# First stage and DeltaNet of an encoder block: tensor work of GpSimd given to VectorE and ScalarE

## The chip, the cores and the metric

The kernel runs on one core of one Trainium2 chip. The metric is device time in microseconds (us), as the median of several runs. Of the kernel before there are three: 1435.29, 1437.44 and 1438.14 us, median 1437.44.

The engines are named as the profile names them: PE is TensorE (matmuls), PEld its weight loads, DVE is VectorE, ACT is ScalarE, POOL is GpSimd, SP is SyncE, which issues nearly all transfers here. Each engine takes its instructions strictly in order; semaphores make one wait for another. An instruction that stands at the head of its engine and waits holds back everything behind it.

## The reference

One encoder block over 256 tokens of width 2048. Two branches read the normalized input: a gated DeltaNet with 8 heads of 128 channels, run forwards and backwards, and a Fourier mixer. Their gated sum goes through an output projection; a squared-ReLU MLP of width 8192 follows. All weights are float32.

```python
h = rms_norm(x, g_mix)
q, k, v, z, f, scal, gates = split(h @ w_in)
q, k, v = split(silu(centred_short_conv(concat(q, k, v), conv_w)))
# per head and direction, in log decay g (<= 0) and beta:
#   S_t = exp(g_t) S_{t-1} (I - beta_t k_t k_t^T) + beta_t v_t k_t^T,  o_t = S_t q_t
y_a = (head_norm(o_fwd + o_bwd) * silu(z)) @ w_dn_up
y_f = real(fft2(f)) @ w_fourier
x = x + (sigmoid(gate_a) * y_a + sigmoid(gate_f) * y_f) @ w_o
x = x + relu(rms_norm(x, g_mlp) @ w_mlp_up) ** 2 @ w_mlp_down
out = rms_norm(x, g_final)
```

## The kernel before

**Weights and precision.** Every weight is streamed from memory once, in tiles of 512 KB (`raw`, four buffers). `split` (L87) turns each into two parts: ACT rounds it to the matmul's format (`hi`, L88), DVE subtracts to get the remainder (`lo`, L92). A product is three matmuls: hi by hi, hi by lo, lo by hi. So each 512 KB costs ACT one instruction of 128x1024, DVE one of 128x1024, and PE 24 matmuls 256 wide or 12 matmuls 512 wide. `pair_fm` (L104) and `tile_fm` (L131) make feature-major tiles, `stream` (L155) makes token-major columns.

**First stage** (`stream_k0`, L224). The transposed input arrives two k-tiles at a time (`xts`). `h_piece` (L188) multiplies it by the norm weights `gm` and splits it (`hh`, both parts); the first four tiles of k are accumulated as the pieces arrive. `h_square` (L203) squares the piece on ACT and adds it on POOL to `acc`, from which `finish_rstd` (L211) makes the reciprocal norms.

**Scalars** (L246 to L307). A small projection gives beta and the decay of each token and head. Softplus is a polynomial on 128x32 elements. Its result `g` is kept in two parts, `g_hi` and `g_lo`.

**DeltaNet.** The heads are done in two groups of four (`dn_group`, L615). In each group `dn_decay` (L425) builds the decay matrices E: eight operand tiles `A` (128x512, the triangular mask U times a per-token scalar, L435) go through matmuls (L436) and an exponential. `dn_k`, `dn_v`, `dn_q` project, convolve (`qkv_chunk`, L310: four dependent instructions on DVE per 128x256, L329) and normalize. `dn_inv` (L446) needs the inverse of unit triangular matrices of 128 rows, 16 per group. It takes their 64 diagonal blocks of 32x32, writes them to memory (`Kc`, L477) and reads them back one per partition (`Mf`, L483), inverts them by back substitution (`Xf`, L486 to L491: 31 steps of a product and a sum), writes `Xf` out (L493) and reads it back as `Xc` (L497). Matmuls then join 32-blocks to 64 (L518 to L529) and 64 to 128 (L537 to L542), giving `DT`. `dn_out` (L557) uses `DT`: a chain of small matmuls (L571, L577, L584, L590, L593, L598) with an eviction on DVE or ACT between each two, and the per-head norm on ACT and POOL.

**What is shared.** The temporary of the substitution, `tf`, has the tag `ti`; so have the temporaries of every second tile of the gate projection (L655), which follows the DeltaNet. The gates' results `merged` occupy the memory of the first group's E, Kt and Y. So the gate tiles can be multiplied into PSUM (four banks), but the first of them leaves PSUM only after the second group's substitution has ended and the first group's `dn_out` has read Y.

**What sets the order.** A scheduler orders each engine's instructions before the run by a simulated timeline (`schedule_with_timeline_sim`, L23). It moves work of one group between that of another. Constants and a few matmuls keep the program's order.

```python
for b in range(31, 0, -1):
    wd = 32 - b
    t3 = tf[:, 0:b * wd].rearrange("p (a c) -> p a c", a=b)
    pool.tensor_tensor(t3, Mf[:, 0:b, b:b + 1].to_broadcast([64, b, wd]),
                       Xf[:, b:b + 1, b:32].to_broadcast([64, b, wd]), op=ALU.mult)
    pool.tensor_tensor(Xf[:, 0:b, b:32], Xf[:, 0:b, b:32], t3, op=ALU.add)
```

## Time and profile before

| | |
|---|---|
| median of three runs | 1437.44 us (1435.29 to 1438.14) |
| span of the profiled execution | 1435.3 us |
| instructions of the program in it | 21399 |
| bytes moved | 255.19 MB, mean 178 GB/s |

The profiled execution has no time of its own beside its span; the span lies 2.1 us below the median and at the lowest of the three runs. What else is used of the profile stands in the prediction. A row of a group gives line, engine, operation, output and inputs, shape and count; then busy time in us, the mean of one in ns, and the idle time before them with what ended it. A row of a timeline gives start and length in us and how many instructions it joins. Durations of neighbouring instructions on one engine overlap a little, so the pitch from start to start is shorter than the duration.

For orientation in time: the first stage ends at 37.7 us; the first group's substitution runs from 119.3 to 184.9 us on POOL, the second group's from 224.3 to 278.3 us; the second z chunk's matmuls (L167) run from 231.8 to 262.3 us; the gate tiles from 267.5 to 386.9 us.

### The profile page before, as it was taken

How to read it: one execution, taken by the hardware profiler on the slowest of the kernel's cores; microseconds unless marked ns; L12 is line 12 of the kernel's file. 1: busy time of each engine (PE TensorE's matmuls, PEld its weight loads, DVE VectorE, ACT ScalarE, POOL GpSimd, SP SyncE). 2: the span in 40 equal slices, each digit the busy share in tenths (PEclk: the TensorE clock that was granted, in tenths of full speed). 3: DMA queues.
4: the chain of work that ended last, by engine and by line, in shares of the span. 5: the costliest groups of instructions: out<-in, count | busy, mean ns of one | idle time of the engine just before them, and what ended most of it. 6: DMA issues, size and time to landing. Idle time of an engine off the chain costs nothing.

```text
span 1435.3 us, 21399 instructions
## 1 busy us (share of the span) xinstructions
PE 1400.2 (98%) x8446; PEld 1235.3 (86%) x8446; DVE 904.4 (63%) x1136; ACT 679.4 (47%) x1017; POOL 189.4 (13%) x241
## 2 busy tenths in 40 slices
PE   8999799899999999999999999999999999999997
PEld 7989789688898899988888888888888888888897
DVE  8898888566655656656566666444446666645553
ACT  5545354455534444445554445333334454434442
POOL 8466926601000000000000000000000000000000
PEclk9999989999999999999999999999999999999999
DMA  7545344344556445576655556666665555666663
GB/s 239 167 155 165 100 136 121 114 139 144 189 179 201 162 158 186 183 257 200 189 182 187 188 187 184 195 196 191 192 192 188 187 186 185 191 191 193 193 198 121
DMA packets 85973, 255.19 MB, mean 178 GB/s; under 512 B 17008, under 2 KB 25200, under 8 KB 85488
## 3 DMA queue, kind: packets, MB, share of 16 engines
q1 hardware_dynamic: 84880, 249.62, 55.8%
q10 hardware_dynamic: 992, 4.19, 0.8%
q8 instruction: 66, 1.08, 0.3%
q14 instruction: 35, 0.29, 0.1%
HBM read 250.64 MB, written 3.15 MB: 177 GB/s over the span
## 4 chain that ended last, share of the span: by engine, by line
PE 83%; POOL 9%; DMA 3%; DVE 2%; issue 2%; ACT 1%; SPq 0%; POOLq 0%; ACTq 0%
PE mm L146 25%; PE mm L145 12%; PE mm L816 8%; PE mm L817 8%; PE mm L818 8%; POOL Xf L491 3%; PE mm L121 3%; PE mm L122 3%; PE mm L127 3%; PE mm L168 3%; PE mm L169 3%; PE mm L167 3%; POOL tf L489 3%; DVE lo L92 1%; DMA raw<-in_w_o_dram 1%
## 5 line engine op out<-in xcount | busy, mean ns | idle before, releaser
L92 DVE TENSOR_TENSOR lo<-raw,hi 128x1024 fp32r<-128x1024 f32 (+1 forms) x459 | 577.1, 1258 | 358.2 <-ACT hi L88 350.9
L88 ACT ACTIVATE hi<-raw 128x1024 fp32r<-128x1024 f32 (+1 forms) x459 | 485.5, 1059 | 436.5 <-PE mm L818 185.8
L146 PE MATMUL mm<-hh,hi 128*128 128x512 f32 x1536 | 539.5, 399 | 3.3 <-ACT hi L88 3.3
L145 PE MATMUL mm<-hh,lo 128*128 128x256 f32 x1440 | 405.8, 282 | 0.9 <-DVE lo L92 0.9
L146 PEld LDWEIGHTS mm<-hh,hi 128*128 128x128 f32 x1536 | 283.8, 189 | 65.0 <-ACT hi L88 3.5
L145 PEld LDWEIGHTS mm<-hh,lo 128*128 128x128 f32 x1440 | 273.1, 190 | 5.2 <-DVE lo L92 1.2
L817 PE MATMUL mm<-lo,rh 128*128 128x512 f32 (+1 forms) x512 | 192.3, 376 | 0.0
L818 PE MATMUL mm<-hi,rl 128*128 128x512 f32 (+1 forms) x512 | 192.3, 376 | 0.0
L816 PE MATMUL mm<-hi,rh 128*128 128x512 f32 (+1 forms) x512 | 173.7, 376 | 0.0
L867 POOL TENSOR_TENSOR rs<-rs,pex 128x1 f32<-128x1 f32 x2 | 1.1, 553 | 1082.0 <-DVE rs L866 1082.0
L818 PEld LDWEIGHTS mm<-hi,rl 128*128 128x128 f32 x512 | 96.4, 188 | 17.6
L816 PEld LDWEIGHTS mm<-hi,rh 128*128 128x128 f32 x512 | 96.2, 188 | 17.5
L817 PEld LDWEIGHTS mm<-lo,rh 128*128 128x128 f32 x512 | 96.3, 188 | 17.3
L127 PE MATMUL mm<-hh,lo 128*128 128x256 f32 x320 | 94.0, 294 | 1.0 <-DVE lo L92 1.0
L122 PE MATMUL mm<-hh,hi 128*128 128x256 f32 x320 | 94.0, 294 | 0.0
L121 PE MATMUL mm<-hh,hi 128*128 128x256 f32 x320 | 93.9, 293 | 0.0
L152 ACT COPY rt<-mm 128x256 f32<-128x256 f32 x64 | 23.9, 373 | 109.1 <-PE mm L146 109.1
L127 PEld LDWEIGHTS mm<-hh,lo 128*128 128x128 f32 x320 | 64.3, 201 | 1.4 <-DVE lo L92 1.2
L122 PEld LDWEIGHTS mm<-hh,hi 128*128 128x128 f32 x320 | 64.5, 202 | 0.5
L121 PEld LDWEIGHTS mm<-hh,hi 128*128 128x128 f32 x320 | 64.5, 202 | 0.2
L153 DVE TENSOR_TENSOR rt<-mm,rt 128x256 f32<-128x256 f32 x64 | 27.2, 425 | 55.6 <-ACT rt L152 55.6
L329 DVE SCALAR_TENSOR_TENSOR y<-u,cw,y 128x256 f32<-128x256 f32 x96 | 58.5, 662 | 3.1 <-ACT y L327 2.9
(314 smaller groups left out, 1928.3 us busy)
## 6 DMA issues: line engine op xcount, KB each, us to landing
raw<-in_w_up_dram SPq DMA_DIRECT2D x128, 512.0 KB, 4.1
raw<-in_w_down_dram SPq DMA_DIRECT2D x128, 512.0 KB, 3.5
raw<-in_w_g_dram SPq DMA_DIRECT2D x64, 512.0 KB, 3.8
raw<-in_w_qkv_dram SPq DMA_DIRECT2D x40, 512.0 KB, 3.9
raw<-in_w_in_dram SPq DMA_DIRECT2D x32, 512.0 KB, 3.8
raw<-in_w_o_dram SPq DMA_DIRECT2D x32, 512.0 KB, 3.9
raw<-in_w_dn_dram SPq DMA_DIRECT2D x16, 512.0 KB, 3.2
raw<-in_w_fo_dram SPq DMA_DIRECT2D x16, 512.0 KB, 3.2
```

The lines of the kernel that those rows point to most:

```text
L88: act.activation(hi, src, AF.Copy, scale=scale)
L92: dve.tensor_tensor(lo, src2, hi.bitcast(F32), op=ALU.subtract)
L121: first = pe.matmul(o, hv[:, cs], ahi[:, k, :], start=(k == 0), stop=False)
L122: pe.matmul(o, hv[:, cs], alo[:, k, :], start=False, stop=False)
L127: end = pe.matmul(o, lv[:, cs], ahi[:, k, :], start=False, stop=(k == nk - 1))
L145: pe.matmul(ps[:, 0:T], lv[:, cs], ab[:, k, 0], start=False, stop=False)
L146: pe.matmul(ps, hv[:, cs], ab[:, k].rearrange("p a b -> p (a b)"), start=(k == 0), stop=(k == KD - 1))
L167: pe.matmul(ps[tb], ah, hi[:, kk, :], start=(k == 0), stop=False)
L329: dve.scalar_tensor_tensor(y[:, j, :], u[:, j, w:w + T], cw[:, cb, w:w + 1], y[:, j, :], op0=ALU.mult, op1=ALU.add)
L816: pe.matmul(ps[tb], ah, hi[:, kk, :], start=(k == 0), stop=False)
L817: pe.matmul(ps[tb], ah, lo[:, kk, :], start=False, stop=False)
L818: pe.matmul(ps[tb], al_, hi[:, kk, :], start=False, stop=(k == 31))
```

## The change

Six pieces of work leave POOL.

- The norm weights: ACT multiplies and rounds in one instruction per k-tile (128x256), and DVE makes the remainder from the input directly, instead of a POOL product (128x512) that ACT and DVE then split.
- The sum of squares `acc` is added on DVE.
- The 29 small instructions of beta, softplus and g go to DVE.
- The decay operands `A`: four ACT instructions of 128x128 with a per-partition scale replace one POOL instruction of 128x512; 64 in all.
- The substitution runs on DVE, and on 128 partitions: each 32x32 block stands on two partitions, one for the even and one for the odd columns of the result, so a step has about half the elements. `Mf` is read back twice (8 transfers instead of 4), `Xf` is 128x512, and it comes back by 8 transfers of 16-element runs instead of 4 of 32-element runs, into `Xh`, from which ACT puts even and odd columns together (`Xc`).
- Comments are dropped, so lines move by a few.

On POOL stay the memsets, the powers, the causal masks, one product of E per group and the small head norm.

```diff
 def h_piece(q):
-    else:
-        pool.tensor_tensor(xg, xt, gm[:, ks].unsqueeze(2).to_broadcast([P, 2, T]), op=ALU.mult)
-        split(h_hi[:, ks, :], h_lo[:, ks, :], xg)
+    for k in range(2 * q, 2 * q + 2):
+        if q == 0:
+            dve.tensor_scalar(h_hi[:, k, :], xts[:, k, :], gm[:, k:k + 1], None, op0=ALU.mult)
+        else:
+            act.activation(h_hi[:, k, :], xts[:, k, :], AF.Copy, scale=gm[:, k:k + 1])
+        dve.scalar_tensor_tensor(h_lo[:, k, :], xts[:, k, :], gm[:, k:k + 1], h_hi[:, k, :].bitcast(F32),
+                                 op0=ALU.mult, op1=ALU.subtract)
 def h_square(q):
-        pool.tensor_tensor(acc, acc, xt, op=ALU.add)
+        dve.tensor_tensor(acc, acc, xt, op=ALU.add)
...
-        pool.tensor_scalar(e3, e3, 2.0 / n, None, op0=ALU.add)
-        pool.tensor_tensor(e3, e3, e2, op=ALU.mult)
+        dve.tensor_scalar(e3, e3, 2.0 / n, None, op0=ALU.add)
+        dve.tensor_tensor(e3, e3, e2, op=ALU.mult)
...
 def dn_decay(gi):
-                    pool.tensor_tensor(A, U, gs.unsqueeze(2).to_broadcast([P, 4, P]), op=ALU.mult)
+                    for h in range(4):
+                        act.activation(A[:, h], (Uf, Ub)[d], AF.Copy,
+                                       scale=gg[:, tb, 8 * d + 4 * gi + h:8 * d + 4 * gi + h + 1].bitcast(F32))
 def dn_inv(gi, kp, E, cn):
-        Mf = pd.tile([64, 32, 32], ...)
-        Xf = pd.tile([64, 32, 32], ...)
+        Mf = pd.tile([P, 32, 32], ...)
+        Xf = pd.tile([P, 32, 16], ...)
-        for b in range(4):
-            nc.sync.dma_start(Mf[16 * b:16 * b + 16], src[b])
+        for r0 in range(0, P, 16):
+            nc.sync.dma_start(Mf[r0:r0 + 16], src[r0 // 16 % 4])
         for b in range(31, 0, -1):
-            wd = 32 - b
-            pool.tensor_tensor(t3, Mf[:, 0:b, b:b + 1].to_broadcast([64, b, wd]),
-                               Xf[:, b:b + 1, b:32].to_broadcast([64, b, wd]), op=ALU.mult)
-            pool.tensor_tensor(Xf[:, 0:b, b:32], Xf[:, 0:b, b:32], t3, op=ALU.add)
+            c0 = b // 2
+            wd = 16 - c0
+            dve.tensor_tensor(t3, Mf[:, 0:b, b:b + 1].to_broadcast([P, b, wd]),
+                              Xf[:, b:b + 1, c0:16].to_broadcast([P, b, wd]), op=ALU.mult)
+            dve.tensor_tensor(Xf[:, 0:b, c0:16], Xf[:, 0:b, c0:16], t3, op=ALU.add)
-        for b in range(4):
-            nc.sync.dma_start(Xc[32 * b:32 * b + 32], back[b])
+        for half in range(2):
+            for b in range(4):
+                nc.sync.dma_start(Xh[32 * b:32 * b + 32, :, half], back[half, b])
+        act.copy(Xc.rearrange("p u (c h) -> p u h c", h=2), Xh)
```

The scheduler places the moved instructions anew. First, DVE while the second group's k is convolved and v is projected (`lo` the remainders of weights, `y` the convolution, `grp` the first group's E). Before:

```order
L92 TENSOR_TENSOR lo_2433<-raw_2431,hi_2432 128x1024
L552 TENSOR_TENSOR grp_521<-grp_521,aux_1666 128x4x128
L324 TENSOR_TENSOR u_1818<-mm_1954,rbc 128x2x256
L92 TENSOR_TENSOR lo_2463<-raw_2461,hi_2462 128x1024
L329 SCALAR_TENSOR_TENSOR y_1821<-u_1818,cw,y_1821 128x256 x6
L92 TENSOR_TENSOR lo_2493<-raw_2491,hi_2492 128x1024
L329 SCALAR_TENSOR_TENSOR y_1821<-u_1818,cw,y_1821 128x256 x2
L92 TENSOR_TENSOR lo_2535<-raw_2533,hi_2534 128x1024
L337 SCALAR_TENSOR_TENSOR y_1821<-th_2086,y_1821 128x1024
L92 TENSOR_TENSOR lo_2565<-raw_2563,hi_2564 128x1024
```

In the changed kernel, at the same place (weight remainders 2509 and 2539 are the counterparts of 2433 and 2463; `tf` and `Xf` belong to the first group's substitution):

```order
L92 TENSOR_TENSOR lo_2509<-raw_2507,hi_2508 128x1024
L487 TENSOR_TENSOR tf_718<-Mf_716,Xf_717 128x81
L404 TENSOR_SCALAR rq_1676<-rq_1676 128x8
L319 TENSOR_TENSOR u_1883<-mm_2019,rbc 128x2x256
L489 TENSOR_TENSOR Xf_717<-Xf_717,tf_718 128x27x3
L487 TENSOR_TENSOR tf_718<-Mf_716,Xf_717 128x78
L92 TENSOR_TENSOR lo_2539<-raw_2537,hi_2538 128x1024
L489 TENSOR_TENSOR Xf_717<-Xf_717,tf_718 128x26x3
L553 TENSOR_TENSOR grp_527<-grp_527,aux_1698 128x4x128
L324 SCALAR_TENSOR_TENSOR y_1886<-u_1883,cw,y_1886 128x256 x2
L553 TENSOR_TENSOR grp_527<-grp_527,aux_1707 128x4x128
L487 TENSOR_TENSOR tf_718<-Mf_716,Xf_717 128x100
```

The 62 instructions of the first substitution now stand one by one between the weight remainders of the second group's k, v, q and z. The first stands behind the seventh of k's eight remainders, the last behind the fifth of z's eight. The transposes that use its result (L502, in the changed kernel L503) stood behind the first remainder of the second group's q, and now stand behind the last of z.

Second, PE in the first group's `dn_out` (L584 there is L585 in the changed kernel). Before, amid the second z chunk (`mm_2979` and `mm_2980` are its two banks):

```order
L167 MATMUL mm_2980<-hi_3000,hh 128x512
L168 MATMUL mm_2980<-lo_3001,hh 128x512
L169 MATMUL mm_2980<-hi_3000,hh 128x512
L167 MATMUL mm_2979<-hi_3018,hh 128x512
L168 MATMUL mm_2979<-lo_3019,hh 128x512
L169 MATMUL mm_2979<-hi_3018,hh 128x512
L167 MATMUL mm_2980<-hi_3018,hh 128x512
L584 MATMUL dn_1717<-rS_1677,DT 128x128 x4
L590 MATMUL dn_1723<-grp_521 128x128
L168 MATMUL mm_2980<-lo_3019,hh 128x512
L169 MATMUL mm_2980<-hi_3018,hh 128x512
```

In the changed kernel, where the second gate tile (`mm_3407`) ends:

```order
L145 MATMUL mm_3407<-hh,lo_3432 128x256
L146 MATMUL mm_3407<-hh,hi_3431 128x512
L542 MATMUL dn_932<-DT,W_78_901 64x64 x8
L572 MATMUL dn_1720<-rho_1213,DT 128x128 x4
L572 MATMUL dn_1727<-rho_1213,DT 128x128 x4
L578 MATMUL dn_1734<-sF_1717,off_665 128x128 x4
L578 MATMUL dn_1743<-sF_1717,off_665 128x128 x4
L585 MATMUL dn_1752<-rS_1718,DT 128x128 x4
L585 MATMUL dn_1758<-rS_1718,DT 128x128 x4
L591 MATMUL dn_1764<-grp_527 128x128
```

and where the third gate tile (`mm_3457`) begins, behind products for the second group (`aux_3237`) and the transposes of the first group's result (L670):

```order
L367 MATMUL aux_3237<-q_3027,k_2154 128x256
L371 MATMUL aux_3237<-q_3028,k_2154 128x256
L372 MATMUL aux_3237<-q_3027,k_2155 128x256
L670 MATMUL aux_4163<-tr,ohat_1716 128x128 x4
L670 MATMUL aux_4174<-tr,ohat_1716 128x128 x4
L146 MATMUL mm_3457<-hh,hi_3459 128x512
L148 MATMUL mm_3457<-hh,lo_3460 128x256
L145 MATMUL mm_3457<-hh,lo_3460 128x256
```

So the whole `dn_out` of the first group moved from between the matmuls of the z chunk to behind it, between the second and the third gate tile, with no weight matmul amid it.

Third, DVE at that same place, in the changed kernel (names with 2246 to 2248 belong to the second group's substitution; before, no instruction of it stood on DVE):

```order
L489 TENSOR_TENSOR Xf_2247<-Xf_2247,tf_2248 128x22x5
L487 TENSOR_TENSOR tf_2248<-Mf_2246,Xf_2247 128x126
L489 TENSOR_TENSOR Xf_2247<-Xf_2247,tf_2248 128x21x6
L487 TENSOR_TENSOR tf_2248<-Mf_2246,Xf_2247 128x120
L580 SCALAR_TENSOR_TENSOR rS_1718<-dn_1734,nea,rho_1213 128x128 x4
L489 TENSOR_TENSOR Xf_2247<-Xf_2247,tf_2248 128x20x6
L580 SCALAR_TENSOR_TENSOR rS_1718<-dn_1743,nea,rho_1213 128x128 x4
L487 TENSOR_TENSOR tf_2248<-Mf_2246,Xf_2247 128x133
L489 TENSOR_TENSOR Xf_2247<-Xf_2247,tf_2248 128x19x7
L487 TENSOR_TENSOR tf_2248<-Mf_2246,Xf_2247 128x126
```

The evictions of the first group's `dn_out` (L580 here) stand between the steps of the second group's substitution.

More of the change, by code (lines that the diff above doesn't have):

```diff
@@ L185, in encoder_block_kernel @@
     scw = pd.tile([P, KD, 64], F32R, tag="sF", name="scw")
-    sqs = pd.tile([P, 2, 2, T], F32, tag="rS", name="sqs")
     def h_piece(q):
-        xt = xts[:, 2 * q:2 * q + 2, :]
-        nc.sync.dma_start(xt, xT[:, 2 * q:2 * q + 2, :])
-        if q == 0:
-            for k in range(2):
-                dve.tensor_scalar(h_hi[:, k, :], xt[:, k, :], gm[:, k:k + 1], None, op0=ALU.mult)
-                dve.scalar_tensor_tensor(h_lo[:, k, :], xt[:, k, :], gm[:, k:k + 1], h_hi[:, k, :].bitcast(F32),
-                                         op0=ALU.mult, op1=ALU.subtract)
-        else:
-            ks = slice(2 * q, 2 * q + 2)
-            xg = sqs[:, q % 2]
-            pool.tensor_tensor(xg, xt, gm[:, ks].unsqueeze(2).to_broadcast([P, 2, T]), op=ALU.mult)
-            split(h_hi[:, ks, :], h_lo[:, ks, :], xg)
+        nc.sync.dma_start(xts[:, 2 * q:2 * q + 2, :], xT[:, 2 * q:2 * q + 2, :])
+        for k in range(2 * q, 2 * q + 2):
[5 more added lines that the diff above has]
+                                     op0=ALU.mult, op1=ALU.subtract)
     def h_square(q):
@@ L271, in encoder_block_kernel @@
     act.activation(nexp, hp[:, 0:16], AF.Exp)
[L272 to L273 removed]
+    dve.tensor_scalar(nexp, nexp, -1.0, None, op0=ALU.mult)
+    dve.tensor_tensor(al, scal[:, :, 16:32], dtb, op=ALU.add)
     e1 = cp.tile([P, 2, 16], F32, name="e1")
@@ L306, in encoder_block_kernel @@
     nea = cp.tile([P, 16], F32, name="nea")
-    pool.tensor_scalar(nea, eab[:, 0:16], -1.0, None, op0=ALU.mult)
+    dve.tensor_scalar(nea, eab[:, 0:16], -1.0, None, op0=ALU.mult)
     def qkv_chunk(c, ps=None):
@@ L477, in dn_inv @@
         nc.sync.dma_start(dscr[gi][0], Kc.rearrange("p u c -> p (u c)"))
-        Mf = pd.tile([64, 32, 32], F32, tag=("sF", "zs1")[gi], name=nm("Mf"))
-        Xf = pd.tile([64, 32, 32], F32, tag=("rS", "ohat1")[gi], name=nm("Xf"))
-        tf = pd.tile([64, 256], F32, tag="ti", name=nm("tf"))
+        Mf = pd.tile([P, 32, 32], F32, tag=("sF", "zs1")[gi], name=nm("Mf"))
+        Xf = pd.tile([P, 32, 16], F32, tag=("rS", "ohat1")[gi], name=nm("Xf"))
+        tf = pd.tile([P, 256], F32, tag="ti", name=nm("tf"))
@@ L481, in dn_inv @@
         src = dscr[gi][0].rearrange("(b a) (u c) -> b u a c", b=4, u=16)
-        for b in range(4):
-            nc.sync.dma_start(Mf[16 * b:16 * b + 16], src[b])
+        for r0 in range(0, P, 16):
+            nc.sync.dma_start(Mf[r0:r0 + 16], src[r0 // 16 % 4])
         pool.memset(Xf, 0.0)
-        pool.memset(Xf.rearrange("p a c -> p (a c)")[:, 0:1024:33], 1.0)
+        for half in range(2):
+            pool.memset(Xf[64 * half:64 * half + 64].rearrange("p a c -> p (a c)")[:, 16 * half:512:33], 1.0)
@@ L486, in dn_inv @@
         for b in range(31, 0, -1):
-            wd = 32 - b
+            c0 = b // 2
+            wd = 16 - c0
             t3 = tf[:, 0:b * wd].rearrange("p (a c) -> p a c", a=b)
-            pool.tensor_tensor(t3, Mf[:, 0:b, b:b + 1].to_broadcast([64, b, wd]),
-                               Xf[:, b:b + 1, b:32].to_broadcast([64, b, wd]), op=ALU.mult)
-            pool.tensor_tensor(Xf[:, 0:b, b:32], Xf[:, 0:b, b:32], t3, op=ALU.add)
-        dxo = dscr[gi][1].rearrange("(u r) n -> u (r n)", r=2)
+            dve.tensor_tensor(t3, Mf[:, 0:b, b:b + 1].to_broadcast([P, b, wd]),
+                              Xf[:, b:b + 1, c0:16].to_broadcast([P, b, wd]), op=ALU.mult)
@@ L493, in dn_inv @@
+            dve.tensor_tensor(Xf[:, 0:b, c0:16], Xf[:, 0:b, c0:16], t3, op=ALU.add)
+        dxo = dscr[gi][1]
         nc.sync.dma_start(dxo, Xf.rearrange("p a c -> p (a c)"))
+        Xh = pd.tile([P, 16, 2, 16], F32, tag="W", name=nm("Xh"))
+        back = dxo.rearrange("(h b u) (a c) -> h b a u c", h=2, b=4, a=32)
+        for half in range(2):
+            for b in range(4):
+                nc.sync.dma_start(Xh[32 * b:32 * b + 32, :, half], back[half, b])
         Xc = pd.tile([P, 16, 32], F32, tag="Kc", name=nm("Xc"))
-        back = dxo.rearrange("(b u) (a c) -> b a u c", b=4, a=32)
```

28 lines of the change are left out of this document (12 added, 16 removed).

## Prediction

> **What bounds the kernel now.** I read the page first, then the table of stretches for the stage that the change touches, then groups by shape, timelines, and the chain of waits. The page's busy times and slices:
>
> ```profile
> PE 1400.2 (98%) x8446; PEld 1235.3 (86%) x8446; DVE 904.4 (63%) x1136; ACT 679.4 (47%) x1017; POOL 189.4 (13%) x241
> PE   8999799899999999999999999999999999999997
> DVE  8898888566655656656566666444446666645553
> POOL 8466926601000000000000000000000000000000
> PEclk9999989999999999999999999999999999999999
> ```
>
> PE is busy nearly throughout: the kernel is bound by matmuls. What it loses lies in the first nine slices, where POOL works and DVE is nearly full. The first 324 us in stretches of 36 us (length, then busy time of each engine, granted clock, DMA share):
>
> ```profile
> core 0: us, PE busy (x) PEld busy (x) DVE busy (x) ACT busy (x) POOL busy (x), PEclk, DMA share, GB/s
> 0.00:36.00 36.00, 29.11 (x204) 27.49 (x205) 29.99 (x23) 21.03 (x31) 30.94 (x30) 1.00 0.72 239
> 36.00:72.00 36.00, 36.00 (x282) 34.94 (x282) 29.25 (x55) 19.50 (x42) 15.88 (x29) 1.00 0.56 169
> 72.00:108.00 36.00, 35.45 (x219) 31.18 (x218) 32.72 (x33) 18.13 (x31) 22.45 (x19) 1.00 0.48 154
> 108.00:144.00 36.00, 34.24 (x274) 34.04 (x273) 31.88 (x41) 18.89 (x37) 22.47 (x32) 0.95 0.54 162
> 144.00:180.00 36.00, 28.46 (x198) 26.86 (x197) 30.58 (x27) 14.34 (x27) 34.33 (x39) 0.91 0.31 103
> 180.00:216.00 36.00, 33.25 (x350) 31.71 (x349) 30.94 (x55) 20.20 (x49) 8.55 (x12) 0.86 0.46 133
> 216.00:252.00 36.00, 36.00 (x275) 33.23 (x274) 31.89 (x45) 15.90 (x25) 25.30 (x32) 1.00 0.46 127
> 252.00:288.00 36.00, 29.57 (x181) 24.30 (x179) 19.86 (x37) 17.08 (x54) 24.36 (x42) 0.91 0.36 108
> 288.00:324.00 36.00, 35.14 (x337) 30.98 (x338) 23.25 (x35) 19.67 (x35) 0.00 (x0) 1.00 0.44 147
> ```
>
> PE's idle time here is 36 less its busy time, summed: 6.9 + 0.55 + 1.76 + 7.54 + 2.75 + 6.43 + 0.86 = 26.8 us. A lower clock costs 36 us times what is missing to 1.00: 1.8 + 3.2 + 5.0 + 3.2 = 13.2 us. So about **40 us** is all that this stage can give back. It has three places: the start (6.9), the stretch 108 to 216 us (idle 12.05, clock 10.0, so 22.1), and 252 to 324 us (idle 7.3, clock 3.2, so 10.5). In between, 36 to 108 us and 216 to 252 us, POOL works as much and PE is full: there its removal is worth nothing.
>
> Why DVE is full: its instructions are longer while POOL reads SBUF. The first row of each pair is a group of the first 360 us; its counterpart is a group of the time after, or an instruction at a moment when POOL is still.
>
> ```profile
> L92 DVE TENSOR_TENSOR lo<-raw,hi 128x1024 fp32r<-128x1024 f32 x88 | 122.9, 1400 | 24.1 <-ACT hi L88 23.2
> L92 DVE TENSOR_TENSOR lo<-raw,hi 128x1024 fp32r<-128x1024 f32 x370 | 453.3, 1225 | 334.3 <-ACT hi L88 327.7
> L329 DVE SCALAR_TENSOR_TENSOR y<-u,cw,y 128x256 f32<-128x256 f32 x96 | 58.5, 662 | 3.1 <-ACT y L327 2.9
> 51.20 0.48 DVE L329 SCALAR_TENSOR_TENSOR y<-u,cw,y 128x256 f32<-128x256 f32 x1
> L92 DVE TENSOR_TENSOR hh<-sqs,hh 128x512 fp32r<-128x512 f32 x7 | 11.4, 1622 | 0.2 <-ACT hh L88 0.2
> 8.90 0.69 DVE L92 TENSOR_TENSOR hh<-sqs,hh 128x512 fp32r<-128x512 f32 x1 [0.15 <-ACT hh L88]
> L337 DVE SCALAR_TENSOR_TENSOR y<-th,y 128x1024 f32<-128x1024 f32 x6 | 10.9, 1812 | 1.2 <-ACT th L336 1.1
> 55.42 1.21 DVE L337 SCALAR_TENSOR_TENSOR y<-th,y 128x1024 f32<-128x1024 f32 x1
> ```
>
> **What DVE gains and takes.** Gains: 88 x 0.175 + 96 x 0.18 + 7 x 0.93 + 6 x 0.60 = 15.4 + 17.3 + 6.5 + 3.6 = 43 us. For what it takes over I need the cost of small instructions:
>
> ```profile
> 61.77 2.47 DVE L329 SCALAR_TENSOR_TENSOR y<-u,cw,y 128x256 f32<-128x256 f32 x6 [1.11 <-ACT y L327]
> 56.55 0.19 DVE L278 SCALAR_TENSOR_TENSOR e<-al 128x32 f32<-128x32 f32 x1
> L491 POOL TENSOR_TENSOR Xf<-Xf,tf 64x31 f32<-64x31 f32 (+15 forms) x62 | 51.0, 822 | 4.2
> L489 POOL TENSOR_TENSOR tf<-Mf,Xf 64x31 f32<-64x31 f32 (+15 forms) x62 | 43.0, 694 | 37.6 <-DMA Mf<-dscr 33.8
> ```
>
> Six dependent ones of 256 elements take 2.47 us, so the pitch is 0.40 us where one lasts 0.48. From 256 to 1024 elements duration grows by (1225 - 480)/768, about 1 ns an element, so the pitch is 0.13 us and 1.04 ns an element. One substitution is 31 steps of two instructions; step b has b x (16 - b/2 rounded down) elements, together 2856, where b x (32 - b) made 5456. So 62 x 0.13 + 5712 x 0.00104 = 14.0 us, **28 us** for both, against 94 us on POOL. The step is not shown by any DVE row; 128x32 in 0.19 us bounds it below (62 x 0.12 + 5.9 = 13.4) and the chopped rows of up to 15 runs could cost as much as 0.2 us each (18.3). [...]
>
> Further: seven square sums at 0.61 (0.69 less the overlap) are 4.3 us; the remainders of h as 14 instructions at 0.40 for 7 at 0.61 are 1.3; 29 scalars at 0.12 are 3.5. In all 37 us. **DVE's total hardly moves** (-6 us); what moves is where it lies and what waits for it.
>
> **Start: -4 us** (0 to -6). Now a pair of k-tiles takes 3.69 us on DVE, the pitch of these two rows:
>
> ```profile
> 12.54 1.78 DVE L92 TENSOR_TENSOR hh<-sqs,hh 128x512 fp32r<-128x512 f32 x1
> 16.23 1.78 DVE L92 TENSOR_TENSOR hh<-sqs,hh 128x512 fp32r<-128x512 f32 x1
> L88 ACT ACTIVATE hh<-sqs 128x512 fp32r<-128x512 f32 x7 | 4.4, 632 | 10.0 <-POOL sqs L200 10.0
> L208 ACT ACTIVATE xts<-xts 128x512 f32<-128x512 f32 x7 | 4.3, 613 | 0.0
> L88 ACT ACTIVATE hi<-raw 128x1024 fp32r<-128x1024 f32 (+1 forms) x459 | 485.5, 1059 | 436.5 <-PE mm L818 185.8
> L606 ACT ACTIVATE tmp<-ohat 128x128 f32<-128x128 f32 x16 | 4.8, 298 | 12.1 <-DVE ohat L601 12.1
> ```
>
> After: DVE 1.15 + 2 x 0.40 + 0.61 = 2.56; ACT 1.06 + 0.61 and two of 128x256 at some 0.5 (between 0.30 for 128 elements and 0.63 for 512) = 2.7; PE's 24 matmuls at 36.00/282 = 0.13 make 3.1. PE is last, 0.6 us a pair sooner, over six or seven pairs 4 us. If transfers (DMA share 0.72) bind instead, nothing.
>
> **36 to 108 us: 0** (to +2). The scalars (3.5 us) and the decay operands (64 x 0.30 = 19 us over both groups) lie beside PE's full stretches; ACT is half idle. The cover ends where PE's decay matmuls come up before their operands.
>
> **First substitution, 108 to 216 us: -16 us** (-20 to -6). POOL's first and last instruction of it:
>
> ```profile
> 119.33 0.25 POOL L489 TENSOR_TENSOR tf<-Mf,Xf 64x31 f32<-64x31 f32 x1 [19.30 <-DMA Mf<-dscr]
> 184.57 0.33 POOL L491 TENSOR_TENSOR Xf<-Xf,tf 64x31 f32<-64x31 f32 x1
> ```
>
> So it holds 65 us, slows DVE all the while, and DVE starves PE. After, DVE has for the 24 weight tiles of v, q and z: 24 x 1.15 = 27.6, twice (16 x 0.40 + two evictions 1.2 + two full-size passes 2.3) = 19.8, the substitution 14, products and evictions some 9: 70 us, against 3 x 192 x 0.128 = 74 us of PE (z is the same bytes). That is 95% full: it fits, but with waits. I leave 6 of the 22.1 us.
>
> **Second substitution with the first group's outputs: +8 us** (0 to +18). The order shows the loss: `dn_out` of the first group no longer has z matmuls around it. From the second to the third gate tile PE has some 80 small matmuls, by the first of these rows (eight in 0.89 us) about 9 us. The second row is one of the three kinds of eviction there.
>
> ```profile
> 317.37 0.89 PE dn L577 x8
> L579 DVE SCALAR_TENSOR_TENSOR rS<-dn,nea,rho 128x128 f32<-128x128 f32 x16 | 4.5, 343 | 0.2 <-PE dn L577 0.2
> ```
>
>  DVE has meanwhile nearly the whole second substitution (13 us), three times eight evictions and norms like these (about 7), products (2.5), three weight remainders (3.5): 26 us. In part they run beside each other: I take it that PE waits some 13 us there, and 5 more where the result comes back through memory and ACT's copy of it stands ahead of the next weight tile. The memory trips before, from the chain of waits:
>
> ```profile
> 115.40 3.77 DMA Mf<-dscr
> 184.93 2.94 DMA dscr<-Xf
> 187.89 3.58 DMA Xc<-dscr
> ```
>
> These three have twice the packets for the `Mf` and `Xh` reads, so between the same and 3.6 us more each; behind the second substitution nothing covers it, and I count 2 of the 5 for it. 18 against 10.5 before is +8.
>
> Sum: -4 + 0 - 16 + 8 = -12. The profiled span of 1435.3 us becomes 1423; the median of the runs is 2.1 us over the span, so **1425 us**.
>
> **Rivals.**
> - *The second place decides, slower* (0.17): DVE, now one queue for weight remainders and substitutions, holds the third gate tile. If the steps cost 0.2 us more each and the memory trips double, the place costs +18, the first substitution gives only 8 and the start 3: +7, 1444 us. It decides once PE's wait between the second and the third gate tile exceeds some 20 us. For it: from 216 to 252 us DVE is 31.89 of 36 us full without any substitution. Against it: the 43 us of relief are sure.
> - *The clock takes it back* (0.10). In 252 to 288 us, 6.4 us of idle time came with 3.2 us of lost clock; 11 us more of idle time at that ratio is 5 us more: 1430. [...]
> - *More comes back* (0.20): `dn_out` and the second substitution overlap so well that the place costs no more than before, and the first gives 20: -4 - 20 + 0 = -24, 1413 us.
> - *Nothing* (0.08): the idle time only moves behind the z chunk, 22 us from one place to the other: 1437 us.
>
> **How the numbers follow.** The forecast has 0.45. Its own range is 1417 to 1433. The range is 1410 to 1442: it takes in most of the better case and part of the slower one. A measurement of this kernel tells 0.2%, 2.9 us. Faster by more than that: 0.45 + 0.20 + 0.10, less 0.02 for what of these ends near zero, 0.73. Same: 0.08 + 0.02 = 0.10. Slower: 0.17.
>
> **What would show it.** Right: weight remainders at 1.23 us throughout; no POOL rows in the substitution; PE full from 10 us to about 35 and idle under 5 us from 108 to 216 us; the largest PE wait in a stretch before the third gate tile, 10 to 15 us, on DVE. A step's pitch near 0.23 us would confirm the 14 us. Wrong: PE still idle 10 us during the first substitution, or its longest wait on the `Mf` read, or on an operand of the decay.

## The result, and the profile after

The changed kernel takes **1413.24 us** (median of 4 runs, 1412.26 to 1414.78) against 1437.79 us for the kernel before (4 runs, 1435.29 to 1438.84): a ratio of 0.9836, 95% interval 0.9822 to 0.985, or 24.5 us less. The profiled span is 1413.1 us, 22.2 less than before. The forecast was 1425 us with a range of 1410 to 1442; the result lies in that range near its lower end, and outside the forecast's own range of 1417 to 1433.

From the page of the changed kernel, the busy times and four of the rows of slices:

```profile
PE 1390.5 (98%) x8446; PEld 1227.3 (87%) x8446; DVE 892.5 (63%) x1303; ACT 702.2 (50%) x1090; POOL 34.9 (2%) x60
PE   9999998799999999999999999999999999999997
DVE  7869998756555666655666666444456666645553
POOL 1001100101000000000000000000000000000000
PEclk9999999899999999999999999999999999999999
```

GpSimd has fallen from 189.4 to 34.9 us. VectorE, which took over most of that work, has gone from 904.4 to 892.5 us: 11.9 us less, where the forecast had 6. Beside the last slice, two dull ones are left on the PE, the seventh and eighth, and only in the eighth is the clock's digit under 9. In stretches of 36 us (length, then busy time and count of each engine, granted clock, DMA share, GB/s):

```profile
core 0: us, PE busy (x) PEld busy (x) DVE busy (x) ACT busy (x) POOL busy (x), PEclk, DMA share, GB/s
0.00:36.00 36.00, 32.80 (x242) 31.94 (x243) 25.86 (x42) 23.48 (x39) 7.15 (x18) 1.00 0.83 279
...
108.00:144.00 36.00, 36.00 (x302) 35.88 (x301) 32.70 (x60) 21.32 (x48) 3.24 (x6) 1.00 0.69 175
144.00:180.00 36.00, 36.00 (x296) 35.68 (x296) 35.38 (x80) 27.29 (x64) 4.38 (x7) 1.00 0.50 162
180.00:216.00 36.00, 35.42 (x209) 30.98 (x207) 33.19 (x65) 18.36 (x33) 2.92 (x1) 1.00 0.62 169
216.00:252.00 36.00, 31.87 (x355) 27.42 (x354) 29.24 (x72) 20.09 (x46) 1.64 (x1) 1.00 0.46 133
252.00:288.00 36.00, 29.39 (x241) 24.44 (x240) 26.29 (x69) 21.18 (x54) 3.82 (x10) 0.86 0.32 88
288.00:324.00 36.00, 36.00 (x295) 32.00 (x294) 20.23 (x33) 16.88 (x27) 0.00 (x0) 1.00 0.37 120
```

From 108 to 216 us the PE now sits idle for 0.58 us at full clock; before it lost 22.1 us there. VectorE is 91 to 98% full in these rows and still starves nobody. What is left stands between 216 and 288 us: 4.13 + 6.61 us idle, and a clock of 0.86 in the second of the two.

The main groups of VectorE in the first 360 us:

```profile
L92 DVE TENSOR_TENSOR lo<-raw,hi 128x1024 fp32r<-128x1024 f32 x95 | 115.7, 1220 | 28.8 <-ACT hi L88 27.8
L324 DVE SCALAR_TENSOR_TENSOR y<-u,cw,y 128x256 f32<-128x256 f32 x96 | 44.1, 503 | 1.3 <-ACT y L322 1.2
L332 DVE SCALAR_TENSOR_TENSOR y<-th,y 128x1024 f32<-128x1024 f32 x6 | 7.3, 1219 | 0.0
```

The weight remainders (L92) take 1220 ns on average instead of 1400, the convolution's steps 503 instead of 662, the activation's last step 1219 instead of 1812: close to the durations that they had before only while GpSimd was still (1225, 480 and 1210 ns).

For the rest of the document the PE's **lost time** is worked out from all matmul records: from each matmul's start to the next one's start, less the usual such time for its line and shape (the 40th percentile of them in that run), summed by place. It takes in idle time, lowered clock and late issue alike, and unlike a sum of idle time and missing clock it counts nothing twice. For before it gives 54.1 us, for after 32.0; the difference, 22.1 us, is within 0.1 us that of the spans.

| us lost by the PE | 0 to 36 | 36 to 126 | 126 to 204 | 204 to 324 | later |
|---|---|---|---|---|---|
| before | 8.3 | 1.6 | 24.0 | 16.4 | 3.8 |
| after | 3.8 | 0.3 | 0.1 | 24.3 | 3.5 |

So the first substitution's stretch gave 23.9 us, the start 4.5 and the stretch between them 1.3, and the second substitution's stretch took back 7.9.

Where that last loss sits, from the timeline of the changed kernel: four rows of the PE and, apart, one of ScalarE (start, length, engine, line, operation; in brackets the idle time ahead and what ended it).

```profile
237.04 0.39 PE L146 MATMUL mm<-hh,hi 128*128 128x512 f32 x1
...
238.16 1.11 PE L542 MATMUL dn<-DT,W 64*64 64x64 f32 x16 [0.72 <-DVE Xf L489]
...
243.22 2.05 PE L578 MATMUL dn<-sF,off 128*128 128x128 f32 x16 [1.63 <-ACT grp L574]
...
264.27 0.79 PE L146 MATMUL mm<-hh,hi 128*128 128x512 f32 x1 [4.36 <-ACT zs L643]
```

```profile
263.54 0.69 ACT L643 ACTIVATE zs<-mm,rstd 128x512 f32<-128x512 f32 x1 [5.11 <-DVE tf L487]
```

The second gate tile's last matmul starts at 237.04 us and the third begins at 264.27, after 27.2 us in which the PE has only small matmuls of `dn_inv` and `dn_out`, a few products and transposes, and their waits. What lets the third begin is ScalarE's eviction of z's second chunk into `zs1` (L643), and what lets that begin is the last step of the second substitution (L487), since the substitution's `Mf` lives in the buffer of `zs1`. The last matmul of that chunk started at 215.9 us, so for 47 us z holds two of the four PSUM banks without adding to them.

### The profile page after: what moved, and what is told of

It reads as the page before. It is cut to its first block, busy times and chain, and to the rows that moved or that the text cites. A ratio compares the mean times of both kernels' runs of the same rounds, so it can differ in the third digit from the quotient of the medians.

```text
span 1413.1 us, 21499 instructions
## 1 busy us (share of the span) xinstructions
PE 1390.5 (98%) x8446; PEld 1227.3 (87%) x8446; DVE 892.5 (63%) x1303; ACT 702.2 (50%) x1090; POOL 34.9 (2%) x60
## 4 chain that ended last, share of the span: by engine, by line
PE 93%; DVE 2%; DMA 1%; issue 1%; ACT 1%; SPq 1%; POOL 0%; POOLq 0%; DVEq 0%; ACTq 0%
PE mm L146 25%; PE mm L145 12%; PE mm L819 8%; PE mm L817 8%; PE mm L818 8%; PE mm L122 5%; PE mm L121 5%; PE mm L127 5%; PE mm L167 4%; PE mm L168 4%; PE mm L169 4%; PE mm L148 1%; DVE lo L92 1%; DMA raw<-in_w_k_dram 1%; PE aux L731 0%
## 5 line engine op out<-in xcount | busy, mean ns | idle before, releaser
L92 DVE TENSOR_TENSOR lo<-raw,hi 128x1024 fp32r<-128x1024 f32 (+1 forms) x459 | 560.4, 1222 | 357.9 <-ACT hi L88 350.8
L146 PEld LDWEIGHTS mm<-hh,hi 128*128 128x128 f32 x1536 | 284.2, 189 | 67.8 <-ACT zs L643 4.6
L122 PE MATMUL mm<-hh,hi 128*128 128x256 f32 x320 | 90.6, 283 | 0.0
L121 PE MATMUL mm<-hh,hi 128*128 128x256 f32 x320 | 90.5, 283 | 0.0
L152 ACT COPY rt<-mm 128x256 f32<-128x256 f32 x64 | 23.9, 373 | 108.8 <-PE mm L146 108.8
L153 DVE TENSOR_TENSOR rt<-mm,rt 128x256 f32<-128x256 f32 x64 | 27.2, 425 | 55.4 <-ACT rt L152 55.4
L121 PEld LDWEIGHTS mm<-hh,hi 128*128 128x128 f32 x320 | 61.3, 192 | 0.3
L122 PEld LDWEIGHTS mm<-hh,hi 128*128 128x128 f32 x320 | 61.3, 191 | 0.3
L127 PEld LDWEIGHTS mm<-hh,lo 128*128 128x128 f32 x320 | 61.2, 191 | 0.2
L168 PE MATMUL mm<-lo,hh 128*128 128x512 f32 x128 | 50.2, 392 | 0.0
L169 PE MATMUL mm<-hi,hh 128*128 128x512 f32 x128 | 50.0, 391 | 0.0
```

The source lines that it names most:

```text
L92: dve.tensor_tensor(lo, src2, hi.bitcast(F32), op=ALU.subtract)
L121: first = pe.matmul(o, hv[:, cs], ahi[:, k, :], start=(k == 0), stop=False)
L122: pe.matmul(o, hv[:, cs], alo[:, k, :], start=False, stop=False)
L127: end = pe.matmul(o, lv[:, cs], ahi[:, k, :], start=False, stop=(k == nk - 1))
L146: pe.matmul(ps, hv[:, cs], ab[:, k].rearrange("p a b -> p (a b)"), start=(k == 0), stop=(k == KD - 1))
L168: pe.matmul(ps[tb], ah, lo[:, kk, :], start=False, stop=False)
```

## The experiments

All twelve leave the kernel's result as it is; e1 and e2 do extra GpSimd work that nothing uses. Ratios are to the kernel before, in runs on the same chip. Lost time of the PE in the start, the first and the second place; the last two columns are the end of the first substitution and the longest gap between two gate matmuls up to 330 us.

| run | median us | ratio, 95% interval | 0-36 | 126-204 | 204-324 | first ends | gap |
|---|---|---|---|---|---|---|---|
| changed | 1413.24 | 0.9836 [0.9822, 0.985] | 3.8 | 0.1 | 24.3 | 200.6 | 27.2 |
| e1 GpSimd reads beside it | 1427.86 | 0.9936 [0.9921, 0.9951] | 2.8 | 13.5 | 25.6 | 214.7 | 27.1 |
| e2 GpSimd writes beside it | 1413.40 | 0.9835 [0.982, 0.9849] | 3.3 | 0.0 | 23.5 | 199.9 | 27.1 |
| e3 both on GpSimd | 1427.40 | 0.9928 [0.9911, 0.9945] | 2.3 | 20.3 | 19.4 | 173.3 | 10.9 |
| e4 own buffers | **1402.37** | 0.9757 [0.9742, 0.9771] | 2.4 | 0.0 | 12.1 | 199.0 | 8.3 |
| e5 substitution alone | 1423.30 | 0.9899 [0.9885, 0.9914] | 8.1 | 2.7 | 22.1 | 202.1 | 21.0 |
| e6 first stage undone | 1417.94 | 0.9869 [0.9855, 0.9884] | 8.5 | 0.0 | 22.9 | 205.2 | 27.0 |
| e7 without the split | 1429.33 | 0.9948 [0.9933, 0.9963] | 3.2 | 0.0 | 41.0 | 222.8 | 54.8 |
| e8 second on GpSimd | 1413.24 | 0.9835 [0.9819, 0.9851] | 3.1 | -0.1 | 22.3 | 199.7 | 26.4 |
| e9 decay on GpSimd | 1429.46 | 0.9943 [0.9928, 0.9958] | 2.9 | 6.8 | 31.0 | 218.1 | 36.7 |
| e10 own buffers, GpSimd | 1426.41 | 0.9916 [0.9899, 0.9933] | 3.6 | 19.7 | 19.3 | 173.9 | 9.6 |
| e11 decay, first group | 1419.42 | 0.9873 [0.9856, 0.9889] | 3.1 | -0.1 | 29.5 | 207.3 | 39.0 |
| e12 decay, second group | 1429.63 | 0.9944 [0.9929, 0.9959] | 2.7 | 6.3 | 33.5 | 220.2 | 46.0 |

### e1 and e2: GpSimd busy beside the first substitution, reading or only writing

```diff
+        if gi == 0:
+            junk = pd.tile([64, 4, 27], F32, tag="junkp", name="junkp")
+            for _ in range(80):
+                pool.tensor_tensor(junk, Mf[0:64, 0:4, 0:27], Mf[0:64, 4:8, 0:27], op=ALU.mult)
         for b in range(31, 0, -1):
```

> The changed kernel with 80 extra GpSimd multiplications (64 partitions x 108 elements, both operands read from Mf, result to a scratch tile nothing else uses) beside the first substitution; the order on the four other engines is that of the changed kernel to the row. Theory A (what the substitution on GpSimd cost was its reading of SBUF beside VectorE): the weight remainders on VectorE go from 1.22 us to about 1.4-1.6 us while these run (some 40 us instead of the old 65), the PE loses 8 to 16 us between 130 and 200 us, time 1421-1430. Theory B (it cost by holding up the small GpSimd steps queued behind it, or by the order of work): VectorE's rows stay at 1.22 us, and the loss, if there is one, is the same as in e2. Theory C (the split on 128 partitions, a shorter chain, brought the gain): 1412-1416, since the chain is unchanged here.

In e2 there is one such multiplication, and behind it:

```diff
+            for _ in range(160):
+                pool.memset(junk, 0.0)
```

> As e1, with one multiplication and 160 GpSimd memsets of the same 64 x 108 scratch tile in its place: GpSimd is as busy at the same place of its queue, but reads no SBUF. Theory A: VectorE's 1.22 us rows stay within 3%, the PE loses under 3 us between 130 and 200 us, time 1412-1417. Theory B: the same loss as in e1. Theory C: 1412-1416.

Measured: 1427.86 and 1413.40 us. VectorE's groups while the extra work runs, first of e1 (128 to 191 us), then of e2 (128 to 172 us), and GpSimd's own group of each; the last row of the first fence is the PE's longest wait in e1 between 108 and 216 us (total, times, longest).

```profile
L324 DVE SCALAR_TENSOR_TENSOR y<-u,cw,y 128x256 f32<-128x256 f32 x30 | 18.0, 633 | 0.0
L319 DVE TENSOR_TENSOR u<-mm,rbc 128x512 f32<-128x512 f32 x3 | 2.0, 678 | 0.0
L486 POOL TENSOR_TENSOR junkp<-Mf 64x108 f32<-64x108 f32 x80 | 52.9, 661 | 11.4 <-DMA Mf<-dscr 5.6
PE mm L127 <- DVE lo L92: 7.1, 5, 3.6
```

```profile
L324 DVE SCALAR_TENSOR_TENSOR y<-u,cw,y 128x256 f32<-128x256 f32 x25 | 11.1, 480 | 0.0
L319 DVE TENSOR_TENSOR u<-mm,rbc 128x512 f32<-128x512 f32 x3 | 2.1, 685 | 0.0
L487 POOL MEMSET junkp<- 64x108 f32 x160 | 29.1, 182 | 8.9
```

With reads, the convolution's steps take 633 ns; with writes 480, as in the changed kernel (475 from 128 to 191 us). L319, which takes one operand from PSUM, is the same in both (678 and 685 ns; 682 in the changed kernel). The PE loses 13.5 us in the first place with reads and nothing with writes, and waits there for weight remainders. The order on the other four engines is that of the changed kernel, so the order isn't behind it. GpSimd's queue can be only a small part: in e1, between 108 and 230 us, VectorE waits for GpSimd twice, for 0.9 us right behind the extra work and for 1.8 us later, in the changed kernel not at all. e2 is no full control for the queue, since its memsets hold GpSimd for 29.1 us and e1's multiplications for 52.9. Theory A holds, B falls but for those 2.7 us, and C falls as a full explanation, since the chain's operations are unchanged here. One detail was expected wrongly: the weight remainders themselves hardly got longer (1260 ns on average from 128 to 191 us, against 1216 in the changed kernel). It is the short instructions around them that did (633 ns against 475), and the remainders came late.

### e3: both substitutions on GpSimd, with the split

```diff
+        eng = pool
...
-            dve.tensor_tensor(t3, ...
+            eng.tensor_tensor(t3, ...
-            dve.tensor_tensor(Xf[:, 0:b, c0:16], ...
+            eng.tensor_tensor(Xf[:, 0:b, c0:16], ...
```

> The changed kernel with only the two substitutions' 124 operations issued by GpSimd, on 128 partitions as changed (half the elements of an operation per partition of the kernel before). Theory A: they take about 0.7 us each, 40-45 us instead of 65 on GpSimd, two thirds of the first place's loss of 22 us comes back (+10 to +16), the second place gives back what it lost (-2 to -6): 1418-1427. Theory C (the shorter chain alone): first place stays full, 1407-1414. If all of the change's gain lies elsewhere: 1413 within 2.

Measured: 1427.40 us, a little past the top of theory A's figure, but only half for its reason. The PE's waits between 108 and 216 us:

```profile
PE dn L520 <- DVE De L504: 11.7, 1, 11.7
PE aux L431 <- ACT offk L556: 1.5, 1, 1.5
```

The first substitution ends at 173.3 us here, 27 us earlier than in the changed kernel, and yet 11.7 of the 20.3 us lost are one wait for its result: the scheduler placed the matmuls that need it earlier still. So the order decides here as much as VectorE's speed, and e3 doesn't measure the contention by itself; e1 does.

### e4: buffers of its own for the second substitution

```diff
-    g = cp.tile([P, 2, 16], F32, name="g")
+    g = e2
-        Mf = pd.tile([P, 32, 32], F32, tag=("sF", "zs1")[gi], name=nm("Mf"))
-        Xf = pd.tile([P, 32, 16], F32, tag=("rS", "ohat1")[gi], name=nm("Xf"))
-        tf = pd.tile([P, 256], F32, tag="ti", name=nm("tf"))
+        Mf = pd.tile([P, 32, 32], F32, tag=("sF", "ohat1")[gi], name=nm("Mf"))
+        Xf = pd.tile([P, 32, 16], F32, tag=("rS", "Kc")[gi], name=nm("Xf"))
+        tf = pd.tile([P, 136], F32, tag="tfs", name=nm("tf"))
```

`g` takes the buffer of `e2`, which is free by then, to make room for `tf`; the longest step has 136 elements.

> The changed kernel with three buffers given out otherwise: the second substitution's Mf in the buffer of ohat1 instead of zs1, its Xf in that of Kc instead of ohat1, its tf in a buffer of its own instead of the gates' ti. So z's second chunk and the gates can be evicted from PSUM while the second substitution still runs. Theory D (the second place's 15.8 us of idle PE and lower clock hang on PSUM banks held by z and the gates until zs1 and ti come free): the stretch without a gate tile (237-265 us) is filled, the PE gets back 5 to 11 us between 216 and 324 us, time 1402-1408. Rival E (VectorE's own queue, 14 us of substitution between the evictions, sets it): the wait moves to other evictions there, 1410-1415.

Measured: 1402.37 us, 0.9757 of before. That is 10.9 us under the changed kernel, and the intervals of the two ratios are apart. The second place by stretches, and the eviction that the third gate tile used to wait for:

```profile
216.00:252.00 36.00, 34.45 (x327) 29.63 (x328) 30.90 (x68) 22.22 (x49) 3.38 (x4) 1.00 0.55 159
252.00:288.00 36.00, 35.01 (x313) 31.07 (x313) 30.28 (x82) 22.48 (x57) 3.69 (x10) 1.00 0.44 124
```

```profile
219.27 0.68 ACT L643 ACTIVATE zs<-mm,rstd 128x512 f32<-128x512 f32 x1
```

The PE is idle for 2.5 us instead of 10.7 there, at full clock, and z's second chunk is evicted at 219 us instead of 263. The substitution itself runs as before, to 266.9 us (263.7 in the changed kernel); VectorE has no less to do (61.2 us busy from 216 to 288 us, against 55.5). Theory D holds: half of the second place's loss (24.3 down to 12.1) hung on buffers that the substitution shared with z and the gates. Which of the three buffers carries it wasn't told apart, and the scheduler laid out the order anew for them, so the 10.9 us are the price of both together. This version beats both kernels.

### e5 and e6: one part alone, one part undone

e5 is the kernel before with `dn_inv` of the changed one (from `Mf` down to `Xc`) and nothing else changed. e6 is the changed kernel with the old `h_piece` and the old last line of `h_square`:

```diff
+            xg = sqs[:, q % 2]
+            pool.tensor_tensor(xg, xt, gm[:, ks].unsqueeze(2).to_broadcast([P, 2, T]), op=ALU.mult)
+            split(h_hi[:, ks, :], h_lo[:, ks, :], xg)
...
-            dve.tensor_tensor(acc, acc, xt, op=ALU.add)
+            pool.tensor_tensor(acc, acc, xt, op=ALU.add)
```

> The kernel before with one part of the change alone: both substitutions on VectorE, split on 128 partitions; norm weights, square sums, per-token scalars and decay operands stay on GpSimd. Theory A: the first place's 22 to 24 us come back (all of them, as in the changed kernel), the second place loses 5 to 8, the start stays as before: 1418-1424. Rival (the parts only work together, since the decay operands on GpSimd still run beside the substitution): the first place gains under 15 us, 1427-1434.

> The changed kernel with the first stage undone: norm weights of h and the adding of squares on GpSimd again, the rest as changed. By the difference of the two starts (PE idle 6.9 us before, 3.2 after): 3 to 5 us slower than the changed kernel, 1415.5-1418.5, all of it ahead of 36 us. Rival (the start's gain is made up later by other waits): within 1 us of 1413.

Measured: 1423.30 and 1417.94 us, both within what was expected. The substitution alone takes 14.0 us off the kernel before (medians 1437.30 and 1423.30 in the same runs) and brings the first place from 24.0 to 2.7 us lost. The first stage is worth 4.7 us, all of it at the start: its first row reads

```profile
0.00:36.00 36.00, 29.60 (x203) 28.19 (x204) 28.06 (x24) 20.80 (x31) 30.39 (x31) 0.95 0.71 238
```

which is 29.60 us of PE work in 36 us against 32.80 in the changed kernel.

### e7: without the split

```diff
-            c0 = b // 2
-            wd = 16 - c0
+            wd = 32 - b
-            dve.tensor_tensor(t3, Mf[:, 0:b, b:b + 1].to_broadcast([P, b, wd]), ...
+            dve.tensor_tensor(t3, Mf[:, 0:b, b:b + 1].to_broadcast([64, b, wd]), ...
```

with the 64-partition tiles and the DMA transfers of the kernel before.

> The changed kernel without the split: the substitutions on VectorE, but on 64 partitions and with the operands, buffers and DMA transfers of the kernel before. Per substitution about twice the elements in as many operations: at the 1.0 ns per element between the 128x78 (238 ns) and 128x126 (288 ns) operations some 5 us more of VectorE. If VectorE's load decides: 3 to 10 us slower than the changed kernel, 1416-1423, more of it in the second place. Rival (what decides is that GpSimd doesn't read SBUF, the split adds nothing): 1411-1415.

Measured: 1429.33 us, 16 us slower than the changed kernel, far over both guesses. The first place is still full (0.0 us lost), so taking GpSimd out is enough there. The second place loses 41.0 us. The PE's longest waits between 216 and 330 us:

```profile
PE mm L146 <- ACT zs L637: 8.3, 1, 8.3
PE dn L513 <- DVE De L497: 6.3, 2, 5.1
```

Without the split both substitutions end later, the first at 222.8 us instead of 200.6, the second at 280.4 instead of 263.7. The result of the first comes late for the small matmuls, and z's banks come free late. The added VectorE time is about 9 us in all (41.4 us of busy time in its 124 operations against 32.4): less than what is lost, since the longer operations stand in VectorE's queue between other work and put off the ends of two chains. The clock adds to it: from 216 to 288 us the PE is idle for 23.3 of the 72 us, and the granted clock is 0.72 and 0.76 in the two halves, against 1.00 and 0.86 in the changed kernel.

### e8: only the second substitution on GpSimd

The edit of e3, for `gi == 1` alone.

> The changed kernel with the second substitution alone on GpSimd (128 partitions); the order on TensorE, ScalarE and in the DMA queue is that of the changed kernel to the row. Rival E (VectorE's queue in the second place is what was lost there): 3 to 8 us faster than the changed kernel, 1405-1410. Theory D (buffers of the second substitution hold PSUM, so that the end of its chain decides): GpSimd's chain is no shorter (34 us against 33), and it takes turns with VectorE: 0 to 8 us slower, 1413-1421.

Measured: 1413.24 us, the changed kernel's time (that it agrees to the hundredth is chance). VectorE is 12.6 us less busy between 216 and 288 us (42.90 against 55.53), and nothing comes of it: the second substitution ends at 261.7 us instead of 263.7, and z is evicted then. Rival E falls: taking VectorE's load away buys nothing as long as the substitution ends as late. That its end matters through the buffers is what e4 shows.

### e9, e11 and e12: the decay operands

```diff
-                    for h in range(4):
-                        act.activation(A[:, h], (Uf, Ub)[d], AF.Copy,
-                                       scale=gg[:, tb, 8 * d + 4 * gi + h:8 * d + 4 * gi + h + 1].bitcast(F32))
+                    gs = gg[:, tb, 8 * d + 4 * gi:8 * d + 4 * gi + 4].bitcast(F32)
+                    U = (Uf, Ub)[d].unsqueeze(1).to_broadcast([P, 4, P])
+                    pool.tensor_tensor(A, U, gs.unsqueeze(2).to_broadcast([P, 4, P]), op=ALU.mult)
```

e9 does so for both groups, e11 for `gi == 0` alone, e12 for `gi == 1` alone.

> The changed kernel with the decay operands undone: 16 GpSimd multiplications of 128x512 (1.15 to 1.48 us each in the kernel before) in place of 64 ScalarE copies of 128x128 (0.39 us each). Theory A (GpSimd reading SBUF takes turns with VectorE): the second group's 8, which run beside the first substitution, hold VectorE up for some 10 us, of which the PE loses 1 to 5 us between 130 and 250 us: 1414-1418. Rival (as in the forecast, the operands are worth nothing on either engine, since ScalarE has the room): within 1.5 us of 1413.

> Half of e9: only the first group's 8 decay operands (36 to 108 us, where the kernel before kept the PE full) on GpSimd, the second group's by ScalarE as changed. Theory F (what counts is which VectorE work they run beside; between 36 and 108 us there is room): within 2.5 us of the changed kernel, 1411-1416. Rival G (they make the first group's chain late, and the second place pays): 5 to 12 us slower, 1418-1425.

> The other half of e9: only the second group's 8 decay operands, which run beside the first substitution, on GpSimd. Theory F: it carries most of e9's 16 us, 10 to 16 us slower than the changed kernel, 1423-1429, with the end of the first substitution some 15 us later. Rival G: 1413-1420.

Measured: 1429.46, 1419.42 and 1429.63 us. e9 was expected at 1414 to 1418 or at 1413, and costs 16.2 us against the changed kernel; it is the largest miss of the twelve. The second group's eight operands carry it alone (e12); the first group's cost 6.2 us by themselves, in the second place and not where they stand, so that theory F is wrong for them and rival G right. Together they cost no more than the second group's alone: the prices don't add, because the scheduler lays out everything behind them anew.

What eight GpSimd operations do to VectorE, from the timeline of e9 (start, length): GpSimd first, then VectorE.

```profile
153.73 6.07 POOL L430 TENSOR_TENSOR A<-tr,g_hi 128x512 fp32r<-128x512 f32 x1
159.77 1.09 POOL L430 TENSOR_TENSOR A<-tr,g_lo 128x512 fp32r<-128x512 f32 x1
```

```profile
158.62 0.28 DVE L487 TENSOR_TENSOR tf<-Mf,Xf 128x133 f32<-128x133 f32 x1
158.83 0.68 DVE L319 TENSOR_TENSOR u<-mm,rbc 128x512 f32<-128x512 f32 x1
159.43 0.53 DVE L489 TENSOR_TENSOR Xf<-Xf,tf 128x133 f32<-128x133 f32 x1
159.88 2.06 DVE L92 TENSOR_TENSOR lo<-raw,hi 128x1024 fp32r<-128x1024 f32 x1
```

A GpSimd operation of a kind that takes 1.09 us right after lasts 6.07 us here, beside eight VectorE instructions in a row, those of 128x1024 at their usual 1.21 us; it ends at 159.80 us, once L319, the first with an operand in PSUM, has run (158.83 to 159.51 us). Beside the next one a weight remainder takes 2.06 us instead of 1.22. And the PE waits for the operand itself: in e12, between 36 and 216 us, the longest wait is

```profile
PE aux L436 <- POOL A L431: 4.0, 1, 4.0
```

The rest of the price is paid in the second place. Over the runs that have the substitution on VectorE and the changed kernel's buffers, its loss goes with the time at which the first substitution ends: 200.6 us and 24.3 lost (changed), 207.3 and 29.5 (e11), 218.1 and 31.0 (e9), 220.2 and 33.5 (e12), 222.8 and 41.0 (e7). Two runs stand off that line: e5, which has all its decay operands on GpSimd and yet ends at 202.1 and loses 22.1, and e1, with 214.7 and 25.6. (In e6, with 205.2 and 22.9, all is later by what the start loses.) So a late first substitution isn't the whole cause. How much of e9's price is VectorE held up, and how much another order of the scheduler, is open: it wasn't tried with the changed kernel's order held fixed.

### e10: e4's buffers and e3's engine together

> The kernel of e4 (own buffers for the second substitution) with both substitutions issued by GpSimd, as in e3. If engine and buffers are two separate matters: the first place loses what it lost in e3 (about 20 us), the second gains what e4 gained against the changed kernel or what e3 lost there (8 to 15 us): 1410-1420. Rival (with z and the gates free of the chain, they fill the first place too, so the engine no longer matters): 1400-1406.

The edit is that of e4 with that of e3. Measured: 1426.41 us, neither of the two. With the substitutions on GpSimd the first place loses 19.7 us as in e3, and the second 19.3, also as in e3: the buffers are worth 1 us here and 10.9 in e4. In this order the matmuls of z's second chunk run until 251 us (in e3 too), where those of the changed kernel and of e4 end at 215 to 216 us: less time is left in which z can hold banks in vain (it is evicted at 270.3 us in e3 and at 263.3 in e10). The PE waits for a result and not for a bank; its longest waits, from 36 to 216 us and from 216 to 330 us:

```profile
PE dn L519 <- DVE De L503: 11.3, 1, 11.3
PE aux L367 <- ACT offk L555: 7.8, 1, 7.8
```

## Why the forecast was too high by 12 us

- **Where the time is lost: right.** All but 0.3 us of the gain came from the first 324 us. What GpSimd's reads cost VectorE was right in place and size: 1400 to 1220 ns, 662 to 503, 1812 to 1219. e1 and e2 show it as cause: reads beside the substitution cost 14.6 us, writes 0.2 us, which is within the noise.
- **Start, -4: right.** Lost time there fell by 4.5 us, and e6 gives 4.7 back.
- **36 to 108 us, 0 (to +2): nearly right in size, wrong as a price.** The PE gained 1.3 us there. But that the decay operands lie beside full stretches of the PE and cost nothing holds only on ScalarE: put back on GpSimd they cost 16.2 us, and the second group's don't lie in this stretch but beside the first substitution. That price belongs to e9's order: e5, which keeps the decay operands and the scalars on GpSimd, is 10.1 us over the changed kernel, and less the 4.7 us of the start (e6) that leaves 5.4 us for both, an estimate.
- **First substitution, -16: this is the step that failed, by its size.** It gave 23.9 us. The forecast left 6 of the 22.1 us, because 70 us of VectorE work against 74 of PE work "fits, but with waits". It fits without any: the scheduler spread the 62 operations over 70 us (130.9 to 200.6, longer than GpSimd's 65) between the weight remainders, and VectorE at 91 to 98% keeps every one in time. How long the substitution takes was not the question; that nothing beside it was stretched was. By e1's price (13.5 us lost for 52.9 us of GpSimd), the 60.8 us that GpSimd was busy between 120 and 185 us before make 15.5; with the 6.3 of e12 some 22, an estimate that counts the operands partly twice, near the 24.0 lost before.
- **The steps' own cost: right.** Their groups in the changed kernel:

```profile
L489 DVE TENSOR_TENSOR Xf<-Xf,tf 128x126 f32<-128x126 f32 (+22 forms) x62 | 16.4, 264 | 1.1
L487 DVE TENSOR_TENSOR tf<-Mf,Xf 128x126 f32<-128x126 f32 (+22 forms) x62 | 16.0, 258 | 5.9 <-DMA Mf<-dscr 4.7
```

  make 32.4 us of busy time for both; from start to start it is a median of 0.295 us where one step follows another and 0.183 where other work stands between them, 64 and 60 of them, so 30 us against the 28 forecast.
- **Second substitution, +8: right in size (+7.9), wrong in reason, so right by luck.** The forecast counted 10.5 us before and 18 after; in lost time it is 16.4 and 24.3, and by the forecast's own measure, idle time and missing clock from 216 to 324 us, 10.5 and 15.8. The forecast had the wait between the second and third gate tile, and the PE does lose 11.9 us from 240 to 264. But its largest single wait there is 4.4 us, for ScalarE's eviction behind the substitution's end, not 10 to 15 us for VectorE; and VectorE's load, which the forecast named as what decides, is refuted: e8 takes the steps off VectorE and gains nothing, e4 leaves them there and gains 10.9 us. What decides, by the rows above and e4, is buffers: z's eviction waits for the last read of `Mf`, so z keeps its PSUM banks. The same wait stood in the profile before:

```profile
278.05 0.69 ACT L642 ACTIVATE zs<-mm,rstd 128x512 f32<-128x512 f32 x1 [2.51 <-POOL tf L489]
```

  The buffer that `tf` shares with the gates was known as well; the forecast put the price on VectorE all the same.
  The memory trips grew as feared, by the chain of waits behind the first substitution, whose last step ends at 200.6 us:

```profile
200.95 4.37 DMA dscr<-Xf
...
206.23 0.49 SPq L496
...
209.27 2.37 DMA Xh<-dscr
```

  The result is back 11.0 us behind the last step, with eight reads issued one after the other at about 0.49 us each (one at 0.87), where it was 6.5 us before. It lies on the chain that leads to the second substitution; what it costs by itself wasn't tried.
- **The rivals.** "More comes back" named the time, 1413, but not the way: the first place gave 23.9 and not 20, and the second did cost its 8, so that hit is luck too. The clock took nothing back on the whole: of the rows up to 324 us one is lowered (0.86), where before there were four. Slower by the second place would have needed a wait over 20 us there: the gap is 27.2 us, but the PE works through more than half of it.
- **The signs.** Three came: weight remainders at 1220 ns, no GpSimd step in the substitution, and 0.58 us idle from 108 to 216 us. Two came in part: from 10 to 35 us the PE is busy for 23.1 of 25 us (19.5 before) and not full, and a step's pitch is 0.24 us by the two medians above. The 40 us that the forecast held to be all there was to gain up to 324 us are 50.3 us in lost time.
